# An encoder layer on one core: where the first three right factors of the down projection are rounded

## The chip, the core and the metric

The kernel runs on one core of a Trainium2 chip. A core has TensorE (PE, with its weight loads as PEld), VectorE (DVE), ScalarE (ACT), GpSimd (POOL) and SyncE (SP); SP only issues DMAs here, and POOL mostly does so too. The engines run on their own and wait for each other by semaphores. The metric is the device time of one execution in microseconds, lower is better.

## What is computed

One layer of a streaming encoder, 512 tokens by 2048 channels, all in float32:

```
h = rms_norm(x, pre_mix_g);  z = h @ w_in                 # q, k, v and u
a = chunked_attention(q, k, v, rel_bias);  p = multiscale_pool(u, pool_w, pool_scale)
x = x + rms_norm(concat([a, p]) @ w_o, post_mix_g)
h = rms_norm(x, pre_ffn_g)
up = causal_dwconv(h @ w_up, conv_w, conv_b)              # 2 x 5632 columns
y = (gelu(up[:, :5632]) * up[:, 5632:]) @ w_down          # 5632 x 2048
x = x + rms_norm(y, post_ffn_g)
```

## The kernel before, in words

**Products in parts.** A float32 factor `v` is split into `hi`, which ACT rounds to the type `fp32r` (L140), and `lo = v - hi`, which DVE subtracts (L141). A product is then hi by hi, hi by lo and lo by hi: three matmuls, which `mm3` issues at L162, L164 and L165. Every weight block thus costs a load, a rounding on ACT and a subtraction on DVE before PE can use it.

**Seven products instead of eight.** The w_o product, most of the up projection and the down projection are computed as seven products of sums of quarter blocks. The products are numbered 1 to 7. Product 1 takes the plain block 11 of the weights, 2 and 3 the plain blocks 21 and 22; 5, 7, 6 and 4 take sums of blocks. For the w_o product (`wo_sum`) and for the first part of the down projection (`first_sum`) these sums are made in DRAM by POOL's DMAs long before.

**The down projection** takes 44 row blocks of w_down in five groups c of eight (4 pairs u each), and a last few blocks apart. A group has fourteen products: column half cc = 0 or 1, product i = 1 to 7; each is 24 matmuls of 512 columns. A right factor (cc, i) is a tile of 128 by 2048, 1 MB, split into `bh` and `bl`; a left factor comes from the gated activations that the up projection has stored in DRAM (`gd`), loaded as `gc` (or `a` for the first) and split into `ah` and `al`. The first group's products are taken in the order (0,1), (1,1), (0,2), (1,2), (0,5), ..., and the planner keeps three factors ahead (`AHEAD`).

**The passage** from up to down projection: the last ten products of the up projection run while the first right factors come in. `next_first` is called after the up product 6 of the last half block and after product 4 of the one before it, and each call brings one right factor, (0,1) and (1,1). The right factors' tiles stand in a pool `pr` that is opened when the left sums of the up projection (`h5`, `h3`, `h6`) are dead, with two tiles each of `raw1` (as loaded), `wh` and `wl`; further rings (`later`) come once the up projection's memory is free. One of the two `raw1` tiles holds the last gated activation, `ca`, from the moment its convolution begins until it has been stored to `gd_last[1]`. By the counter of `right_tile`, ring numbers 0 to 3 of `raw1` all come from `pr`.

**What was special of the first three.** (0,1), (1,1) and (0,2) (`READY`) were split amid the w_o products: `ready_blocks` loaded each in two halves (`rw`, L843), rounded them, and stored hi and lo to DRAM (`rw01h` and so on, L850), one step after each quarter of a w_o product other than product 1. At the passage POOL then loaded the finished `bh` and `bl` (L1110); no engine had to split them.

**What sets the order.** PE's order is the program's own. On every other engine a scheduler fixes the order of the instructions when the program is built, by priorities and its own estimates; on the chip each engine then works strictly in that order and waits where it must. Loads on SP also stand in one order.

Of the kernel before, what the change touches and what calls it, by code (L numbers as in the profile page):

```python
# [9 lines left out]
F32 = mybir.dt.float32  # L10
F32R = mybir.dt.float32r
# [4 lines left out]
P = 128  # L16
S = 512
# [14 lines left out]
CU = 4  # L32
# [13 lines left out]
def f32(ap):  # L46
    return ap.bitcast(F32)
# [34 lines left out]
def encoder_layer(ctx: ExitStack, tc: tile.TileContext, x, xT, vecs, rel, post_mix, post_ffn,  # L82
# [7 lines left out]
    nc = tc.nc  # L90
# [7 lines left out]
    dram = ctx.enter_context(tc.tile_pool(name="dram", bufs=1, space=bass.MemoryType.DRAM))  # L98
# [7 lines left out]
    def bank(name):  # L106
        return psum.tile([P, 512], F32, tag="ps", name=name)
# [30 lines left out]
    def split(hi, lo, src, scale=None):  # L138
        if scale is None:
            rounded = nc.scalar.activation(hi, src, AF.Copy)  # L140
            rest = nc.vector.tensor_sub(lo, src, f32(hi))  # L141
        else:
            rounded = nc.scalar.activation(hi, src, AF.Copy, scale=scale)
            rest = nc.vector.scalar_tensor_tensor(lo, src, scale, f32(hi), op0=ALU.mult, op1=ALU.subtract)
        split.last, split.rest = rounded.ins, rest.ins
        return rounded.ins
# [14 lines left out]
    def mm3(ps, l, r, first, last, onto=False):  # L161
        nc.tensor.matmul(ps, l[0], r[0], start=first, stop=False, skip_group_check=onto)  # L162
        low = ps if len(r[1].shape) == 2 else ps.rearrange("p (a b) -> p a b", a=2)
        nc.tensor.matmul(low, l[0], r[1], start=False, stop=False, skip_group_check=onto)  # L164
        nc.tensor.matmul(ps, l[1], r[0], start=False, stop=last, skip_group_check=onto)  # L165
# [41 lines left out]
    def part(w, *idx):  # L207
        return tuple(v[(slice(None),) + idx] for v in w)
# [47 lines left out]
    def first_block(cc, j, l):  # L256
        cs = slice(l * D // 2 + cc * S, l * D // 2 + (cc + 1) * S)
        return w_down[:2 * P * CU, cs].rearrange("(u j p) n -> p u j n", j=2, p=P)[:, :, j, :]

    READY = (0, 1), (1, 1), (0, 2)  # L260
    ready_w = {at: [dram.tile([P, CU, S], F32, name=f"rw{at[0]}{at[1]}{p}") for p in "hl"] for at in READY}

    ready_parts = [(at, j) for at in READY for j in range(2)]

    specs = v_specs(0)
    FIRST_PART = len(specs)
# [21 lines left out]
    first_sum = {i: [dram.tile([P, CU, S], F32, name=f"t{i}{cc}") for cc in range(2)] for i in (5, 7, 6, 4)}  # L288
# [63 lines left out]
    for kb in range(KD):  # L352
        i, o = divmod(kb, 8)
        nc.sync.dma_start(xt[kb // 4][:, kb % 4, :], xT[kb * P:(kb + 1) * P, :])
        for n, what in enumerate("qk"):
            if kb in chunks:
                raw, hi, lo = first[f"{what}0_{i}"]
# [5 lines left out]
        for what in "qk":  # L363
            _, hi, lo = first[f"{what}0_{i}"]
# [248 lines left out]
    with tc.tile_pool(name="p1", bufs=2, reuse_waits="tile") as p1:  # L613
# [222 lines left out]
                split(*(w[:, 4 * i:4 * i + 4, :] for w in parts), v)  # L836
            return parts

        def ready_blocks():
            for at, j in ready_parts:  # L840
                v, hi = (p2.tile([P, 1024], dt, tag=tag, name=tag) for tag, dt in (("rw", F32), ("rwh", F32R)))
                lo = v.bitcast(F32R)
                nc.sync.dma_start(v.rearrange("p (a b) -> p a b", a=2),  # L843
                                  first_block(at[0], at[1] - 1, 0)[:, 2 * j:2 * j + 2, :])
                for _ in range(4):
                    yield
                split(hi, lo, v)
                yield
                for dest, part_ in zip(ready_w[at], (hi, lo)):
                    nc.sync.dma_start(dest[:, 2 * j:2 * j + 2, :], f32(part_).rearrange("p (a b) -> p a b", a=2))  # L850
                for _ in range(3):
                    yield

        ready_steps = ready_blocks()

        wo_banks = [bank(f"m{n}") for n in range(8)]
        ONTO = 6, 3, 7, 4

        def wo_product(i, cc, left, between=None):
            at = 2 * cc + (4 if i in (2, 5, 3) else 0)  # L860
            ps = wo_banks[at:at + 2]
            for q in range(4):
                w = weights.get(f"wo{i}_{cc}_{q}")
                for j in range(2):
                    kb = 2 * q + j
                    for t in range(2):
                        mm3(ps[t], tuple(v[:, kb, t * P:(t + 1) * P] for v in left), part(w, j),
                            i not in ONTO and kb == 0, kb == 7, i in ONTO)
                if i != 1:
                    next(ready_steps, None)  # L870
                if between:
                    between(q)
            return ps
# [9 lines left out]
    with tc.tile_pool(name="p2", bufs=1, reuse_waits="tile") as p2:  # L883
# [38 lines left out]
        for cc in range(2):  # L922
            add_out(y11, cc, wo_product(2, cc, a12))
# [147 lines left out]
    gd_last = [dram.tile([P, 2, S], F32, name=f"gd{u}") for u in (NU - 2, NU - 1)]  # L1071
# [7 lines left out]
    later, turns = {}, {}  # L1079

    def right_tile(tag, name, dt=F32R):

        n = turns[tag] = turns.get(tag, -1) + 1
        if later and n % (2 + LATER[tag]) >= 2:
            return later[tag](name, dt)
        return pr.tile([P, CU, S], dt, tag=tag, bufs=2, name=name)
# [3 lines left out]
    def raw1(name, dt=F32):  # L1090
        return right_tile("raw1", name, dt)

    def right(c, cc):

        def load(j, l):
            b = later["raw2"](f"b{j}{l}") if j else raw1(f"b{j}{l}")
            r, cs = 256 * CU * c, slice(l * C + cc * S, l * C + (cc + 1) * S)
            nc.sync.dma_start(b, w_down[r:r + 256 * CU, cs].rearrange(
                "(u j p) n -> p u j n", j=2, p=P)[:, :, j, :])
            return b  # L1100

        b = {}
        order = yield
        while True:
            i = order
            if (c, (cc, i)) in ready_first:
                hi, lo = right_tile("wh", "bh"), right_tile("wl", "bl")
                for v, source in zip((hi, lo), ready_w[cc, i]):
                    with tc.issue_after(first_right.part) if first_right.part else nullcontext():
                        first_right.part = nc.gpsimd.dma_start(v, source.bitcast(F32R)).ins  # L1110
                order = yield hi, lo
                continue
            if c == 0:

                v = first_right(cc, i, raw1 if (ORDER0.index((cc, i)) - len(ready_first)) % 5 < 3 else later["raw2"])
            else:
                for jl in {1: (11, 12), 6: (22,), 2: (21,)}.get(i, ()):
                    b[jl] = load(jl // 10 - 1, jl % 10 - 1)
                if i == 5:
                    nc.vector.tensor_add(b[11], b[11], b[12])  # L1120
                if i == 7:
                    nc.vector.tensor_add(b[12], b[22], b[12])
                if i == 6:
                    nc.vector.tensor_add(b[11], b[11], b[22])
                if i == 4:
                    nc.vector.tensor_add(b[21], b[21], b[11])  # L1126
                v = b[{1: 11, 5: 11, 7: 12, 6: 11, 2: 21, 3: 22, 4: 21}[i]]
            hi, lo = right_tile("wh", "bh"), right_tile("wl", "bl")
            split(hi, lo, v)
            order = yield hi, lo  # L1130

    def first_right(cc, i, ring):

        v = ring(f"t{i}")
        source = first_sum[i][cc] if i in first_sum else first_block(cc, *{2: (1, 0), 3: (1, 1)}[i])
        with tc.issue_after(first_right.last) if first_right.last else nullcontext():
            first_right.last = nc.sync.dma_start(v, source).ins
        return v

    first_right.last = first_right.part = None  # L1140
    ready_first = [(0, at) for at in READY]

    ORDER = 1, 5, 6, 3, 7, 2, 4
    ORDER0 = tuple((cc, i) for i in (1, 2, 5, 6, 3, 7, 4) for cc in range(2))
# [352 lines left out]
    with tc.tile_pool(name="p4", bufs=2, reuse_waits="tile") as p4:  # L1497
        def ring(tag, shape, n):
            return lambda name, dt=F32: p4.tile([P, *shape], dt, tag=tag, bufs=n, name=name)

        raw2 = later["raw2"] = ring("raw2", (CU, S), 2)
# [66 lines left out]
        def next_product():  # L1568
            c, cc, i, l, r = ready.pop(0)
            multiply(cc, i, l, r)  # L1570
            keep_product(c, cc, i)

        for f in factors():
            ready.append(f)
            if firsts:
                firsts.pop(0)
                with tc.issue_after(split.last):
                    keep_product(0, len(ready) - 1, 1)
            if len(ready) == 2 and product.last is not None:
                with tc.issue_after(first_right.part):  # L1580
                    nc.gpsimd.dma_start(gd_last[1], product.last)
                product.last = None
            if len(ready) > AHEAD:
                next_product()
# [93 lines left out]
        for n in ("11", "12", "21", "22"):  # L1678
            for t in range(2):
                at = y[t + 2 * int(n[0]) - 2]  # L1680
                l = int(n[1]) - 1
                load_sum(n, t, at[:, l * C:(l + 1) * C])
                if n in not_stored:
                    v = at[:, l * C + S:(l + 1) * C]
# [60 lines left out]
```

## Time and profile before

| | us |
|---|---|
| median of 3 timed runs | 1860.05 (1859.49 to 1861.0) |
| the profiled execution, its own time | 1858.89 |
| span of the profiled execution, first to last instruction | 1857.1 |
| PE busy | 1842.6 (99% of the span) |
| DVE busy | 1532.2 (83%) |
| ACT busy | 1084.4 (58%) |
| POOL busy | 302.8 (16%) |
| mean granted clock of PE | 0.999 of full speed |

Times in the trace count from the first instruction. A PE row of 0.39 us does not mean that a matmul takes the array so long: successive matmuls of 512 columns start 0.227 us apart and overlap. "[2.70 <- X]" behind a row is the time for which that engine sat idle before it, and who ended the wait. An idle engine other than PE costs nothing as long as PE does not wait for it.

### The profile page before, as it was taken

How to read it: one execution, taken by the hardware profiler on the slowest of the kernel's cores; microseconds unless marked ns; L12 is line 12 of the kernel's file. 1: busy time of each engine (PE TensorE's matmuls, PEld its weight loads, DVE VectorE, ACT ScalarE, POOL GpSimd, SP SyncE). 2: the span in 40 equal slices, each digit the busy share in tenths (PEclk: the TensorE clock that was granted, in tenths of full speed). 3: DMA queues.
4: the chain of work that ended last, by engine and by line, in shares of the span. 5: the costliest groups of instructions: out<-in, count | busy, mean ns of one | idle time of the engine just before them, and what ended most of it. 6: DMA issues, size and time to landing. Idle time of an engine off the chain costs nothing.

```text
span 1857.1 us, 25452 instructions
## 1 busy us (share of the span) xinstructions
PE 1842.6 (99%) x9598; PEld 1584.3 (85%) x9598; DVE 1532.2 (83%) x1799; ACT 1084.4 (58%) x1376; POOL 302.8 (16%) x402
## 2 busy tenths in 40 slices
PE   9999999999999999999999999999999999999998
PEld 7888888888879888888888888888888888888886
DVE  6988778878588988888887888888887899899876
ACT  7654455456564666566565665666655655565553
POOL 3411001100000112212122122121121001111101
PEclk9999999999999999999999999999999999999999
DMA  8599977998987798888888988889888977777785
GB/s 319 171 319 302 322 230 233 267 264 310 326 308 202 185 220 195 205 204 200 201 200 203 207 202 195 204 206 205 199 179 288 363 224 171 193 211 178 176 230 157
DMA packets 139338, 426.01 MB, mean 229 GB/s; under 512 B 11920, under 2 KB 15376, under 8 KB 133520
## 3 DMA queue, kind: packets, MB, share of 16 engines
q0 software_dynamic: 54864, 173.56, 45.8%
q1 hardware_dynamic: 84352, 250.84, 38.8%
q8 instruction: 75, 1.23, 0.3%
q14 instruction: 47, 0.39, 0.1%
HBM read 370.35 MB, written 104.33 MB: 256 GB/s over the span
## 4 chain that ended last, share of the span: by engine, by line
PE 69%; DMA 1%; DVE 1%; issue 0%; ACT 0%; DVEq 0%; POOLq 0%; ACTq 0%
PE qa L170 16%; PE qa L176 8%; PE qg L170 8%; PE qg L176 4%; PE qd L170 4%; PE pa L162 4%; PE pa L165 4%; PE pa L164 4%; PE qd L176 2%; PE pg L162 2%; PE pg L165 2%; PE pg L164 2%; PE up L165 1%; PE up L162 1%; PE up L164 1%; PE pd L164 1%
## 5 line engine op out<-in xcount | busy, mean ns | idle before, releaser
L140 ACT ACTIVATE wfh<-wx 128x1024 fp32r<-128x1024 f32 x192 | 203.4, 1059 | 154.3 <-PE qg L170 54.4
L170 PE MATMUL qa<-gT,wfh 128*128 128x512 f32 x1152 | 288.6, 392 | 0.0
L141 DVE TENSOR_TENSOR wfl<-wx,wfh 128x1024 fp32r<-128x1024 f32 x192 | 234.6, 1222 | 61.0 <-ACT wfh L140 44.0
L170 PEld LDWEIGHTS qa<-gT,wfh 128*128 128x128 f32 x1152 | 207.2, 189 | 37.1
L1362 POOL DMA_DIRECT2D wx<-in_w_up x122 | 104.6, 858 | 502.6 <-DVE wfl L141 467.9
L140 ACT ACTIVATE wfh<-wy 128x1024 fp32r<-128x1024 f32 x96 | 101.7, 1060 | 108.5 <-PE qg L170 57.2
L170 PE MATMUL qg<-h,wfh 128*128 128x512 f32 x656 | 162.2, 389 | 0.1
L176 PE MATMUL qa<-gT,wfl 128*128 128x256 f32 x1152 | 161.4, 283 | 0.6 <-ACT zm L1422 0.6
L176 PEld LDWEIGHTS qa<-gT,wfl 128*128 128x128 f32 x1152 | 151.5, 191 | 4.9 <-ACT zm L1422 0.8
L170 PEld LDWEIGHTS qg<-h,wfh 128*128 128x128 f32 x656 | 122.9, 188 | 25.9 <-ACT zb L1418 0.5
L141 DVE TENSOR_TENSOR bl<-b,bh 128x2048 fp32r<-128x2048 f32 x56 | 127.2, 2285 | 19.1 <-ACT bh L140 11.7
L140 ACT ACTIVATE bh<-b 128x2048 fp32r<-128x2048 f32 x56 | 106.0, 1911 | 52.8 <-DVE b L1126 21.8
L141 DVE TENSOR_TENSOR wfl<-wy,wfh 128x1024 fp32r<-128x1024 f32 x96 | 117.1, 1220 | 12.6 <-ACT wfh L140 7.8
L162 PE MATMUL pa<-bh,ah 128*128 128x512 f32 x320 | 124.5, 389 | 0.0
L164 PE MATMUL pa<-bl,ah 128*128 128x512 f32 x320 | 124.5, 389 | 0.0
L165 PE MATMUL pa<-bh,al 128*128 128x512 f32 x320 | 124.5, 389 | 0.0
L141 DVE TENSOR_TENSOR wfl<-wz,wfh 128x1024 fp32r<-128x1024 f32 x48 | 58.7, 1223 | 54.2 <-PE qa L170 54.2
L176 PEld LDWEIGHTS qg<-h,wfl 128*128 128x128 f32 x656 | 89.5, 190 | 6.4
L170 PE MATMUL qd<-gT,wfh 128*128 128x512 f32 x384 | 94.9, 389 | 0.0
L176 PE MATMUL qg<-h,wfl 128*128 128x256 f32 x656 | 91.5, 282 | 0.0
L170 PEld LDWEIGHTS qd<-gT,wfh 128*128 128x128 f32 x384 | 71.9, 188 | 14.9
L170 PE MATMUL qa<-h,wfh 128*128 128x512 f32 x328 | 82.1, 392 | 0.0
(554 smaller groups left out, 4352.5 us busy)
## 6 DMA issues: line engine op xcount, KB each, us to landing
wx<-in_w_up POOLq DMA_DIRECT2D x122, 512.0 KB, 6.2
b<-in_w_down SPq DMA_DIRECT2D x32, 1024.0 KB, 7.0
wt<-in_w_o POOLq DMA_DIRECT2D x24, 1024.0 KB, 16.8
wx<-in_w_up SPq DMA_DIRECT2D x43, 512.0 KB, 5.5
wz<-in_w_up SPq DMA_DIRECT2D x41, 512.0 KB, 5.7
wy<-in_w_up SPq DMA_DIRECT2D x41, 512.0 KB, 4.7
wy<-in_w_up POOLq DMA_DIRECT2D x41, 512.0 KB, 6.7
sum<-part POOLq DMA_DIRECT2D x38, 512.0 KB, 6.4
```

The lines of the kernel that those rows point to most:

```text
L140: rounded = nc.scalar.activation(hi, src, AF.Copy)
L141: rest = nc.vector.tensor_sub(lo, src, f32(hi))
L162: nc.tensor.matmul(ps, l[0], r[0], start=first, stop=False, skip_group_check=onto)
L164: nc.tensor.matmul(low, l[0], r[1], start=False, stop=False, skip_group_check=onto)
L165: nc.tensor.matmul(ps, l[1], r[0], start=False, stop=last, skip_group_check=onto)
L170: nc.tensor.matmul(ps, w[0][:, kb], pairs[kb][0], start=fresh and not kb, stop=last, skip_group_check=not fresh)
L176: nc.tensor.matmul(ps[:, sl], w[1][:, kb], pair[:, sl], start=False, stop=last, skip_group_check=not fresh)
L1362: nc.gpsimd.dma_start(self.raw[k, what], self.block(k, m, kh), accum_op=ALU.add)
```

## The change

The three early factors lose their special way. `READY`, `ready_w`, `ready_blocks` and the call in `wo_product` go, with six loads, six roundings, six subtractions and twelve stores of half a factor. At the passage POOL's six loads of finished halves go, and (0,1), (1,1), (0,2) go through `first_right` and `split` like the other eleven: one load of 1 MB on SP, one rounding, one subtraction each. The choice of ring (`raw1` or `raw2`) now counts from the first factor and not from the fourth. The store of the last gated activation no longer stands behind POOL's loads.

```
-    READY = (0, 1), (1, 1), (0, 2)
-    ready_w = {at: [dram.tile([P, CU, S], F32, name=f"rw{at[0]}{at[1]}{p}") for p in "hl"] for at in READY}
...
-        def ready_blocks():
-            for at, j in ready_parts:
-                v, hi = (p2.tile([P, 1024], dt, tag=tag, name=tag) for tag, dt in (("rw", F32), ("rwh", F32R)))
...
-                if i != 1:
-                    next(ready_steps, None)
...
-            if (c, (cc, i)) in ready_first:
-                hi, lo = right_tile("wh", "bh"), right_tile("wl", "bl")
-                for v, source in zip((hi, lo), ready_w[cc, i]):
-                    with tc.issue_after(first_right.part) if first_right.part else nullcontext():
-                        first_right.part = nc.gpsimd.dma_start(v, source.bitcast(F32R)).ins
-                order = yield hi, lo
-                continue
             if c == 0:
-                v = first_right(cc, i, raw1 if (ORDER0.index((cc, i)) - len(ready_first)) % 5 < 3 else later["raw2"])
+                v = first_right(cc, i, raw1 if ORDER0.index((cc, i)) % 5 < 3 else later["raw2"])
...
-        source = first_sum[i][cc] if i in first_sum else first_block(cc, *{2: (1, 0), 3: (1, 1)}[i])
+        source = first_sum[i][cc] if i in first_sum else first_block(cc, *{1: (0, 0), 2: (1, 0), 3: (1, 1)}[i])
...
             if len(ready) == 2 and product.last is not None:
-                with tc.issue_after(first_right.part):
-                    nc.gpsimd.dma_start(gd_last[1], product.last)
+                nc.gpsimd.dma_start(gd_last[1], product.last)
```

PE's order is the same in both programs. Amid the w_o products, on DVE, from the last quarter of product (6,1) on (`wo_..l` is the low part of a w_o block, `y` the product's rows, `small` the norm's statistics, `x` the new residual), before:

```order
L906 TENSOR_TENSOR y_4118<-m_3901,y_4118 128x512
L141 TENSOR_TENSOR rw<-rw,rwh 128x1024
L141 TENSOR_TENSOR wo_0_3l<-wo_0_3r,wo_0_3h 128x1024
L915 TENSOR_TENSOR y_4118<-y_4118,gain 128x2x512
L952 TENSOR_REDUCE small<-small 128x2
```

and after:

```order
L882 TENSOR_TENSOR y_4112<-m_3895,y_4112 128x512
L141 TENSOR_TENSOR wo_0_3l<-wo_0_3r,wo_0_3h 128x1024
L891 TENSOR_TENSOR y_4112<-y_4112,gain 128x2x512
L928 TENSOR_REDUCE small<-small 128x2
L929 TENSOR_SCALAR small<-small 128x2
```

The subtraction `rw` that stood between the product's addition and the next low part is gone; the rest keeps its order.

SP's queue at the passage, before (`t` is a right factor as loaded, `gc` and `a` left factors; the digit behind `t` is the product):

```order
L1455 DMA a_13117<-gd0_0_5654 128x4x256
L1137 DMA t2_13308<-in_w_down 128x4x512
L1521 DMA gc0_13299<-gd0_0_5654 128x2048
L1137 DMA t5_13318<-t50_108 128x2048
L1521 DMA gc1_13324<-gd0_1_5655 128x2048
```

and after:

```order
L1423 DMA a_13071<-gd0_0_5606 128x4x256
L1106 DMA t1_13065<-in_w_down 128x4x512
L1106 DMA t1_13107<-in_w_down 128x4x512
L1106 DMA t2_13251<-in_w_down 128x4x512
L1489 DMA gc0_13257<-gd0_0_5606 128x2048
L1106 DMA t2_13266<-in_w_down 128x4x512
L1106 DMA t5_13276<-t50_102 128x2048
L1489 DMA gc1_13282<-gd0_1_5607 128x2048
```

Three loads, (0,1), (1,1) and (0,2), now stand ahead of (1,2)'s and of both loads of left factors `gc`.

DVE's queue at the passage, before (`z` and `RR` belong to the up projection's results, `ca`, `cb`, `cx` to the convolution):

```order
L141 TENSOR_TENSOR al<-a,ah 128x1024
L1437 TENSOR_TENSOR z<-qa_12801,z 128x256
L1438 TENSOR_TENSOR z<-z,RR 128x1024
L1427 TENSOR_TENSOR zm<-zb,zm 128x512
L1207 SCALAR_TENSOR_TENSOR ca<-z,vec,ca 128x511 x2
L1208 SCALAR_TENSOR_TENSOR ca<-z,vec,ca 128x510 x2
```

and after, two pieces (rows between them left out by "..."):

```order
L141 TENSOR_TENSOR al<-a,ah 128x1024
L1405 TENSOR_TENSOR z<-qa_12753,z 128x256
L1406 TENSOR_TENSOR z<-z,RR 128x1024
L141 TENSOR_TENSOR bl<-t_13065,bh 128x2048
L1175 SCALAR_TENSOR_TENSOR ca<-z,vec,ca 128x511 x2
...
L1406 TENSOR_TENSOR z<-z,RR 128x1024
L141 TENSOR_TENSOR bl<-t_13107,bh 128x2048
L1175 SCALAR_TENSOR_TENSOR cb<-z,vec,cb 128x511
...
L1198 TENSOR_TENSOR ca<-ca,cx 128x512
L141 TENSOR_TENSOR bl<-t_13251,bh 128x2048
L141 TENSOR_TENSOR al<-gc_13257,ah 128x1024
L141 TENSOR_TENSOR bl<-t_13266,bh 128x2048
```

Three subtractions of 2048 columns now stand among the last convolutions, and `al` of the second left factor stands behind the third of them; the three roundings stand at the same places of ACT's queue.

## Rows read from the trace of the kernel before

**Rows 1.** The page, its first part: busy time of each engine, share, instructions.

```profile
PE 1842.6 (99%) x9598; PEld 1584.3 (85%) x9598; DVE 1532.2 (83%) x1799; ACT 1084.4 (58%) x1376; POOL 302.8 (16%) x402
```

**Rows 2.** PE's waits from 380 us on: line, waited for: us in total, times, longest.

```profile
PE m L164 <- DVE wo_1l L141: 2.7, 1, 2.7
PE pd L164 <- DMA bl<-rw02l: 0.6, 1, 0.6
PE qa L176 <- ACT zm L1422: 0.6, 1, 0.6
```

**Rows 3.** Order of time, PE: start us, us, line, out<-in [idle before].

```profile
518.91 0.50 PE L164 MATMUL m<-wo_1l,s 128*128 128x512 f32 x1 [2.70 <-DVE wo_1l L141]
```

**Rows 4.** The same, ACT and then DVE, ahead of that wait.

```profile
505.93 1.06 ACT L140 ACTIVATE rwh<-rw 128x1024 fp32r<-128x1024 f32 x1 [5.84 <-DMA rw<-in_w_down]
...
507.02 1.23 DVE L141 TENSOR_TENSOR rw<-rw,rwh 128x1024 fp32r<-128x1024 f32 x1 [4.36 <-ACT rwh L140]
...
512.86 4.86 DVE L967 SCALAR_TENSOR_TENSOR x<-y,small,x 128x1024 f32<-128x1024 f32 x4
517.64 1.21 DVE L141 TENSOR_TENSOR wo_1l<-wo_1r,wo_1h 128x1024 fp32r<-128x1024 f32 x1
```

**Rows 5.** By tile: the removed pieces, duration ns min/median/max, first and last start.

```profile
L140 ACT ACTIVATE rwh<-rw x6: 1059/1061/1062, 424.5 to 505.9; 128x1024 fp32r<-128x1024 f32 x6
L141 DVE TENSOR_TENSOR rw<-rw,rwh x6: 1219/1226/1229, 425.6 to 507.0; 128x1024 fp32r<-128x1024 f32 x6
...
L1110 POOL DMA_DIRECT2D bh<-rw01h x1: 817/817/817, 1404.3 to 1404.3; - x1
```

**Rows 6.** By tile: the added pieces' kind, as eleven other factors have it.

```profile
L140 ACT ACTIVATE bh<-t x11: 1900/1917/1933, 1429.4 to 1478.8; 128x2048 fp32r<-128x2048 f32 x11
L141 DVE TENSOR_TENSOR bl<-t,bh x11: 2280/2285/2293, 1431.5 to 1484.1; 128x2048 fp32r<-128x2048 f32 x11
```

**Rows 7.** Order of time, ACT and DVE at the passage.

```profile
1415.19 0.39 ACT L1436 ACTIVATE z<-qa 128x256 f32<-128x256 f32 x1 [0.83 <-PE qa L170]
...
1416.78 1.23 DVE L1438 TENSOR_TENSOR z<-z,RR 128x1024 f32<-128x1024 f32 x1
```

**Rows 8.** Order of time, PE: the first down products (0,1), (1,1), (0,2), (0,5).

```profile
1423.29 0.39 PE L162 MATMUL pa<-bh,ah 128*128 128x512 f32 x1
...
1428.96 0.39 PE L164 MATMUL pa<-bl,ah 128*128 128x512 f32 x1
...
1435.49 0.39 PE L165 MATMUL pd<-bh,al 128*128 128x512 f32 x1
...
1446.41 0.39 PE L165 MATMUL pg<-bh,al 128*128 128x512 f32 x1
```

**Rows 9.** DMA issues, each of one short stretch: KB, median us to landing.

```profile
b<-in_w_down SPq DMA_DIRECT2D x1, 1024.0 KB, 5.8
...
DMA to landing us min/median/max: 5.8/7.0/9.8
...
b<-in_w_down SPq DMA_DIRECT2D x1, 1024.0 KB, 6.7
gc<-gd SPq DMA_DIRECT2D x1, 1024.0 KB, 8.7
...
t<-t SPq DMA_DIRECT2D x1, 1024.0 KB, 4.8
...
t<-in_w_down SPq DMA_DIRECT2D x1, 1024.0 KB, 10.5
```

**Rows 10.** By stretch: us, busy of PE, PEld, DVE, ACT, POOL, clock, DMA, GB/s.

```profile
1411.00:1420.00 9.00, 9.00 (x50) 7.81 (x49) 7.16 (x10) 4.62 (x7) 0.00 (x0) 1.00 1.06 419
```

**Rows 11.** The same, at PE's one wait amid w_o and behind its last matmul.

```profile
516.00:519.00 3.00, 0.30 (x2) 0.09 (x1) 3.00 (x4) 0.76 (x2) 0.00 (x0) 1.00 0.80 259
...
1852.00:1857.00 5.00, 0.00 (x0) 0.00 (x0) 1.68 (x4) 0.00 (x0) 0.00 (x0) 0.50 0.58 210
```

## What I predict

> **What bounds the kernel now.** I read the page's busy times first: TensorE works for 1842.6 us of a span of 1857.1 [rows 1]. A change can therefore do two things: fill what little PE still waits, or make PE wait anew. The list of PE's waits from the w_o products to the end has three lines: 2.7 us for `wo_1l`, 0.6 for the stored `bl` of (0,2), 0.6 for `zm` in the up projection [rows 2]. The change touches the first two. All it can win is thus 2.7 + 0.6 = 3.3 us, 0.18% of the time. What it can lose has no such limit, so most of the working is about the passage.
>
> **The w_o products: what goes.** In order of time PE stands still for 2.70 us before the second matmul on `wo_1l`, up to 518.91 [rows 3]. Followed backwards [rows 4]: DVE made `wo_1l` at 517.64, directly behind the new residual `x`, which it began at 512.86 and which took 4.86 us. DVE had come late to `x`, since it had waited 4.36 us for `rwh`, and ACT 5.84 us for the last half factor `rw` from DRAM. Both engines work strictly in their order, so ACT's rounding `rwh` of 1.06 us and DVE's subtraction `rw` of 1.23 held up all that was queued behind them. The new order lacks both. DVE's work behind them then begins at once; the wait of 4.36 and the 1.23 of the piece itself go, of which the other waits of the norm take back a little: I put `wo_1l` some 5 us earlier, at 512.5. PE needs it at 518.91 − 2.70 = 516.2. The margin of 3.7 us makes the wait vanish whole: **−2.7 us**. If something else were last there, between 0 and 2.7 would be kept; the top is excluded from being more, since no other wait stands there.
>
> The other pieces removed are six roundings of 1.06 us and six subtractions of 1.23 us, spread from 424.5 to 507 [rows 5], six loads and twelve stores on SP and six loads on POOL. I cost them at nothing: PE's list shows no wait near them but the one just counted, so PE's own products cover them; the stores gate nobody but POOL's loads at the passage.
>
> **The passage: what comes.** Three roundings of 1.92 us on ACT, three subtractions of 2.29 us on DVE (the duration of eleven other factors' [rows 6]) and three loads of 1 MB on SP. As 4.2 us of engine work per factor beside products of 24 × 0.227 = 5.4 us this would hide. What matters is where loads may start. `pr` has two `raw1` tiles. One holds `ca` until the last gated activation is stored. So (0,1), (1,1) and (0,2), ring numbers 0, 1 and 2, all come through the other tile, and each load must wait until DVE's `bl` of the factor before has read it. SP works in order, so the load of `gc0`, which stands behind (0,2)'s, waits as well. It is a chain of load, rounding, subtraction, load, rounding, subtraction.
>
> *Factor (0,1).* POOL's load of its stored half started at 1404.3, when the up projection's memory was free [rows 5]; I take no later a start for the new load. With any landing time of the rows below it is there ahead of ACT's place for it, behind `z` at 1415.19 [rows 7]: rounded by 1417.5. DVE's place for it is behind the addition that starts at 1416.78 and takes 1.23: `bl` from 1418.0 to 1420.3. PE takes it at 1423.29 [rows 8], so it costs nothing; 3 us of margin.
>
> *Load time.* This is the one large unknown: L, from issue to landing of 1 MB from w_down on SP. The kernel loads the same tiles all through the down projection: alone 5.8 us at the least, 7.0 in the median, up to 9.8 [rows 9]. One load of another source landed after 4.8, and the load of (1,2) at the passage took 10.5 [rows 9], in a stretch in which DMA moved 419 GB/s [rows 10]. That traffic was largely POOL's 6 MB of stored halves, which the change takes away, and at 1420 and 1430 only one load is open, because the next may not start. I take 5.9; ends 4.8 and 10.5.
>
> *Factor (1,1).* Load from 1420.3 to 1426.2, `bh` to 1428.1, `bl` to 1430.4. PE's second matmul of the product wants `bl` at 1428.96 [rows 8]: **1.4 us** of wait, part of the next sum.
>
> *Factor (0,2).* Load from 1430.4 to 1436.3, `bh` to 1438.2, `bl` to 1440.5. The left factor `gc0` is queued directly behind; in the pair of rows where a 1 MB load and a `gc` follow each other they took 6.7 and 8.7 us [rows 9], so it lands some 2.4 us after the factor, 1438.7, and `ah` is ready at 1439.8, `al` behind DVE's `bl` at 1441.6. Before, the third matmul of that product, the first to use `al`, ran at 1435.49 [rows 8]. Thus **+6.1 us** in all, the 1.4 included and the old 0.6 for `rw02l` replaced. In L the sum is 1420.3 + 2 L + 9.5, so each microsecond of L counts twice.
>
> *Factors (1,2) and (0,5).* They no longer wait for one slot; loads of 1 MB then land some 2.5 us apart. (1,2) lands near 1441.5 and is rounded by 1443.6, 2 us ahead of its product. Behind it DVE has two `bl`, three pieces of 1024 columns and two of 512 before the `al` of (0,5): 4.6 + 3.7 + 1.4 = 9.7, so 1453.3 less overlaps of 0.1 each, 1452.8 to 1453.1. Due is the row of 1446.41 [rows 8] plus 6.1 = 1452.5: about **+0.5 us**. From there PE takes 5.4 us a factor while ACT, DVE and the loads need 2 to 4.6, so the lead is rebuilt and nothing is late again. ca's convolution ends some 4 us later on DVE, but its consumer, a later product, is no earlier due.
>
> **The clock.** With the new waits PE does almost nothing from about 1435.7, the end of (1,1)'s product, to 1439.9, and runs two matmuls until 1441.6. [...] Hence +1.5 in place of +0.5.
>
> **Sum.** −2.7 + 6.1 + 1.5 = **+4.9 us**. The profiled execution had 1858.89 and its span 1857.1; it would come to 1863.8. It lies 1.2 below the median of the runs, 1860.05, so the forecast on that scale is **1865.0 us**.
>
> [...] The rows give 5.8 to 5.9 us for an undisturbed load of 1 MB [rows 9]. [...]
>
> **The rivals.**
> - *The clock holds.* The two matmuls between and the short gaps keep it at 1.00. −2.7 + 6.1 + 0.5 = +3.9: 1864.0. For it: the 2.70 us at 516 did nothing. Against: this gap is longer. Chance 0.22.
> - *Quick loads.* One row shows 4.8 us [rows 9]. With L = 4.8 the stall is 6.1 − 2 × 1.1 = 3.9, and PE's gap shrinks to that of 516, which left the clock alone: −2.7 + 3.9 = +1.2, 1861.3. [...] For quick loads: DMA is nearly idle then. Against: not one of the w_down loads came under 5.8. Chance 0.14.
> - *The other side: the stall is hidden.* If loads of (1,1) and (0,2) need not wait for DVE's `bl`, because the slot is free earlier than I think, all three land ahead of PE and only the gains stay: −2.7 to −3.3, 1857.4 to 1856.8. It decides where L falls to 5.9 − 3.4 / 2 = 4.2 us, where stall and gain are equal. Against: two tiles, `ca` in one. Chance 0.06, and most of it lies within 0.2%.
> - *The w_o wait stays.* If another load or the norm's own chain makes `wo_1l` late, the 2.7 is not won: +7.6, 1867.6. Chance 0.08. The change not doing what it says would be this case too.
> - *Dear loads.* At the median of 7.0 [rows 9] the stall grows by 2.2: +7.1, 1867.1. At the 10.5 of the passage's own load it grows by 9.2: +14.1, 1874. For it: the row of 10.5 was taken in this very stretch. Against: its company is gone. Chance 0.10.
>
> **How the numbers follow.** The forecast with the clock falling has 0.40; the five rivals 0.22, 0.14, 0.06, 0.08 and 0.10. A measurement of this kernel tells 0.2%, 3.7 us, from no change: below 1856.3 is faster, above 1863.8 slower. Faster needs more than the gains that exist, so 0.03 for what I have not seen. Slower: the forecast (its price of the clock could be 0 and L 5.8, so 0.34 of its 0.40), 0.15 of the 0.22 that the clock holds, the last two whole, and little else: 0.68. Same: 0.29. The range runs from 1861.0, which cuts off the hidden stall and half of the quick loads, to 1868.5, which takes in the w_o wait and loads of 7 us and cuts off the dearest.
>
> **What the profile after would show.** PE's wait for `wo_1l` near 516 is gone. SP's loads of `t1` start near 1404 and 1420.3 and the first of `t2` near 1430.4, each directly at the end of a `bl`, with 5.8 to 6 us to landing. PE waits about 1.4 us for the `bl` of (1,1), then 4 to 5 us for `ah` and `al` of `gc0`. The clock by stretches reads less than 1.00 a little behind 1440. I am wrong if the load of (1,1) starts before 1420 (another slot), if L is far from 5.9, or if PE's wait at 516 has a new releaser.

## The result and the profile after

The changed kernel takes 1866.9 us in the median (1863.93 to 1869.13, 6 runs), the kernel before beside it 1860.37. The ratio is 1.0035 with an interval of 1.0022 to 1.0047: **slower by 6.5 us**, where +4.9 was forecast (1865.0, range 1861.0 to 1868.5). A second set of runs (after_again below) gave 1.0018 (1.0008 to 1.0028), 1864.23 against 1860.65. One execution of each of the two kernels in that set took 3085 us, at a mean granted clock of 0.556, and is left out of the ratio. Slower holds in both sets; the size is less certain, since the two intervals together reach from 1.5 to 8.7 us.

The profiled execution took 1866.7, its span is 1864.9 against 1857.1. The page's first part, to set beside [rows 1]:

```profile
PE 1847.7 (99%) x9598; PEld 1587.5 (85%) x9598; DVE 1533.1 (82%) x1796; ACT 1084.4 (58%) x1373; POOL 300.7 (16%) x396
```

PE has the same 9598 matmuls and is busy 5 us longer: a first sign that they ran slower, since no work was added. PE's waits from 380 us on, to set beside [rows 2]:

```profile
PE pd L162 <- ACT ah L140: 3.4, 1, 3.4
PE pa L164 <- DVE bl L141: 1.8, 1, 1.8
PE pd L165 <- DVE al L141: 0.6, 1, 0.6
PE pg L165 <- DVE al L141: 0.4, 1, 0.4
PE qa L176 <- ACT zm L1390: 0.3, 1, 0.3
```

The wait for `wo_1l` is gone; four new ones stand at the first down products. In order of time, PE at the place of [rows 3] and at those of [rows 8]:

```profile
516.13 0.40 PE L164 MATMUL m<-wo_1l,s 128*128 128x512 f32 x1
...
1419.99 0.39 PE L162 MATMUL pa<-bh,ah 128*128 128x512 f32 x1
...
1427.87 0.50 PE L164 MATMUL pa<-bl,ah 128*128 128x512 f32 x1 [1.82 <-DVE bl L141]
...
1438.43 0.50 PE L162 MATMUL pd<-bh,ah 128*128 128x512 f32 x1 [3.44 <-ACT ah L140]
...
1439.76 0.79 PE L165 MATMUL pd<-bh,al 128*128 128x512 f32 x1 [0.61 <-DVE al L141]
...
1441.21 0.63 PE L165 MATMUL pd<-bh,al 128*128 128x512 f32 x1
...
1445.05 0.63 PE L165 MATMUL pd<-bh,al 128*128 128x512 f32 x1
...
1454.20 0.50 PE L165 MATMUL pg<-bh,al 128*128 128x512 f32 x1 [0.39 <-DVE al L141]
```

DVE began `wo_1l` 5.2 us earlier than in [rows 4]:

```profile
512.43 1.22 DVE L141 TENSOR_TENSOR wo_1l<-wo_1r,wo_1h 128x1024 fp32r<-128x1024 f32 x1
```

PE reaches (0,1) 3.3 us earlier than before (1423.29) and the third matmul of (0,2) 4.3 later (1435.49). The rows 1441.21 and 1445.05 are nine matmuls apart, 0.427 us each and not 0.227; the granted clock reads 0.50 there, as the steps from 1440 on show below. The third matmul of (0,5) is 7.8 later (1446.41), and so it stays to the end.

The chain behind these waits, in ACT's and DVE's rows of the same stretch:

```profile
1423.57 1.92 ACT L140 ACTIVATE bh<-t 128x2048 fp32r<-128x2048 f32 x1 [2.60 <-DMA t<-in_w_down]
...
1434.34 1.91 ACT L140 ACTIVATE bh<-t 128x2048 fp32r<-128x2048 f32 x1 [7.44 <-DMA t<-in_w_down]
1437.32 1.06 ACT L140 ACTIVATE ah<-gc 128x1024 fp32r<-128x1024 f32 x1 [1.07 <-DMA gc<-gd]
...
1414.63 2.29 DVE L141 TENSOR_TENSOR bl<-t,bh 128x2048 fp32r<-128x2048 f32 x1
...
1425.53 2.29 DVE L141 TENSOR_TENSOR bl<-t,bh 128x2048 fp32r<-128x2048 f32 x1 [2.23 <-ACT bh L140]
...
1436.28 2.29 DVE L141 TENSOR_TENSOR bl<-t,bh 128x2048 fp32r<-128x2048 f32 x1 [4.62 <-ACT bh L140]
1438.49 1.22 DVE L141 TENSOR_TENSOR al<-gc,ah 128x1024 fp32r<-128x1024 f32 x1
```

The first `bl` ends at 1416.9, the second at 1427.8. SP's loads of (1,1) and (0,2) were issued at 1416.94 and 1427.84, each at the end of the `bl` before it. SP's own waits from 1385 to 1436 us name the same releaser for both; below that line stands their time to landing, each load taken in a short stretch:

```profile
SPq L1106 <- DVE bl L141: 19.9, 2, 15.6
...
t<-in_w_down SPq DMA_DIRECT2D x1, 1024.0 KB, 6.6
...
t<-in_w_down SPq DMA_DIRECT2D x1, 1024.0 KB, 6.5
```

And the granted clock (the third figure from the end) in steps of 5 us: it fell twice, behind the wait of 1.8 us and behind the long one.

```profile
1425.00:1430.00 5.00, 3.17 (x11) 2.06 (x10) 4.47 (x5) 1.90 (x3) 0.00 (x0) 0.88 0.13 32
1430.00:1435.00 5.00, 4.98 (x18) 3.68 (x16) 1.67 (x3) 0.66 (x1) 0.56 (x1) 0.78 0.99 295
1435.00:1440.00 5.00, 0.96 (x3) 0.61 (x4) 3.43 (x2) 3.28 (x4) 0.00 (x0) 0.91 1.00 380
1440.00:1445.00 5.00, 5.00 (x12) 3.89 (x13) 2.01 (x1) 3.95 (x4) 0.00 (x0) 0.50 1.03 434
1445.00:1450.00 5.00, 5.00 (x21) 4.04 (x20) 3.03 (x3) 0.73 (x1) 0.00 (x0) 0.91 1.02 429
```

### The profile page after: what moved, and what is told of

The parts are those of the page before. It is cut to its first block, busy times and chain, and to the rows that moved or that the text cites. A ratio compares the mean times of both kernels' runs of the same rounds, so it can differ in the third digit from the quotient of the medians.

```text
span 1864.9 us, 25394 instructions
## 1 busy us (share of the span) xinstructions
PE 1847.7 (99%) x9598; PEld 1587.5 (85%) x9598; DVE 1533.1 (82%) x1796; ACT 1084.4 (58%) x1373; POOL 300.7 (16%) x396
## 4 chain that ended last, share of the span: by engine, by line
PE 93%; DMA 3%; DVE 2%; ACT 1%; issue 1%; SPq 0%; DVEq 0%; POOLq 0%; ACTq 0%
PE qa L170 18%; PE qa L176 10%; PE qg L170 9%; PE qg L176 5%; PE qd L170 4%; PE pa L165 4%; PE pa L164 4%; PE pa L162 4%; PE m L162 3%; PE m L165 3%; PE m L164 3%; PE qd L176 2%; PE pg L165 2%; PE pg L164 2%; PE pg L162 2%; PE v L164 2%
```

## The experiments

All of them are read by the same three distances between PE's rows in the trace, in us: the w_o products (first to last matmul), (0,1) (its first matmul) to (0,2) (its third), and from there to the third matmul of (0,5). Without a wait and at a granted clock of 1.00 they are 158.7 (after), 11.3 (two_stored) and 10.9 (before). What lies ahead of them is left out: PE's first w_o matmul stands between 389.3 and 392.6 us in these fourteen traces, so spans of single traces differ by up to 3.4 us before the change can tell. Beside them the timed median, that of the kernel before in the same set, and the ratio with its interval.

| kernel | w_o | to (0,2) | to (0,5) | median, before | ratio |
|---|---|---|---|---|---|
| before | 161.6 | 12.2 | 10.9 | | |
| before_again | 164.9 | 11.8 | 10.9 | 1859.85, 1860.94 | 0.9994 (0.9980 to 1.0007) |
| after | 158.7 | 19.8 | 14.4 | 1866.9, 1860.37 | 1.0035 (1.0022 to 1.0047) |
| after_again | 158.7 | 19.0 | 12.5 | 1864.23, 1860.65 | 1.0018 (1.0008 to 1.0028) |
| wo_alone | 158.7 | 15.4 | 10.9 | 1859.09, 1860.62 | 0.9999 (0.9986 to 1.0012) |
| wo_alone_2 | 158.7 | 15.8 | 12.3 | 1854.62, 1860.65 | 0.9975 (0.9965 to 0.9985) |
| passage_alone | 164.0 | 19.1 | 13.6 | 1869.71, 1860.62 | 1.0050 (1.0036 to 1.0064) |
| other_ring | 158.7 | 14.4 | 11.6 | 1858.0, 1860.62 | 0.9989 (0.9979 to 0.9999) |
| no_link | 158.7 | 14.7 | 11.6 | 1860.13, 1860.62 | 0.9999 (0.9990 to 1.0008) |
| two_links | 158.7 | 14.7 | 13.2 | 1859.81, 1860.65 | 0.9999 (0.9991 to 1.0008) |
| in_pieces | 158.7 | 13.1 | 11.6 | 1856.82, 1860.94 | 0.9973 (0.9963 to 0.9984) |
| clock_held | 158.7 | 19.2 | 12.4 | 1862.96, 1860.65 | 1.0014 (1.0005 to 1.0023) |
| two_stored | 160.2 | 11.3 | 11.5 | 1854.64, 1860.94 | 0.9960 (0.9942 to 0.9977) |
| two_stored_lead | 158.7 | 11.3 | 11.5 | 1855.84, 1861.57 | 0.9970 (0.9959 to 0.9981) |

**The two halves of the change, each alone.** First the w_o part, on the kernel before:

```
-                if i != 1:
-                    next(ready_steps, None)
...
-                for v, source in zip((hi, lo), ready_w[cc, i]):
+                for v, source in zip((hi, lo), [first_block(cc, i - 1, 0)] * 2):
```

> One part of the change alone. The loads, roundings, subtractions and stores of the three factors amid the w_o products are gone, the passage is as before: POOL loads six finished halves (it reads w_down unsplit as both halves, so the values of the three first down products are not the layer's, the work is). My theory: the only thing won in the w_o products is PE's wait of 2.70 us for wo_1l, and it is not given back later, so 1860.4 - 2.7 to 3.0 = 1857.4 to 1857.7. The rival that the wait comes back elsewhere (the up projection, the passage): 1860.4. PE's list of waits tells them apart: no wait near 516, and 0.6 us for bl at the passage as before.

The w_o products took their 158.7 us, but the passage lost 3.2 to two waits that the edit itself brought, and the time is that of before:

```profile
PE pa L164 <- DMA bl<-in_w_down: 1.8, 1, 1.8
PE pd L164 <- DMA bl<-in_w_down: 1.7, 1, 1.7
```

So its time, where 1857.4 to 1857.7 was expected, tells nothing of the sum. It was repeated with `(first_sum[5][cc], first_sum[6][cc])` as sources:

> Again the w_o part alone, with the fault of wo_alone mended: there POOL read the rows of w_down in pieces and came late (waits of 1.8 and 1.7 us for bl that the kernel before hasn't). Here it reads whole tiles of the same layout as the stored halves (the sums t5 and t6, so the values of the three first down products are not the layer's). My theory: no wait at 516, 0 to 0.6 us of wait at the passage, 2.7 to 3.3 us below the kernel before. Rival (the gain of the w_o products is given back): no difference.

The ratio of 0.9975 is 4.6 us, the medians lie 6.0 apart: more than forecast, although the profiled execution of this kernel, one of its slowest, waited 4.0 us for POOL's last load. The other half, the passage of the changed kernel with the early steps still in place:

```
-                v = first_right(cc, i, raw1 if (ORDER0.index((cc, i)) - len(ready_first)) % 5 < 3 else later["raw2"])
+                v = first_right(cc, i, raw1 if ORDER0.index((cc, i)) % 5 < 3 else later["raw2"])
...
-    ready_first = [(0, at) for at in READY]
+    ready_first = []
...
```

> The other part alone. The three factors are still loaded, rounded, subtracted and stored amid the w_o products (nobody reads the stores), and the passage is that of the changed kernel. My theory: the two parts add up, so the wait of 2.7 us at 516 stands and the passage costs the same as in the changed kernel: 1866.9 + 2.7 to 3.0 = 1869.6 to 1869.9. Rival: the passage's loss depends on what was won before (the clock or the loads fall differently): 1866.9 or less. Also looked at: the granted clock behind the 2.70 us wait at 516, against the clock behind the wait of 1.8 us at the passage.

It came to 1869.7, as said. Its 9.3 us (ratio 1.0050) less 4.6 are 4.7, between the two measurements of the whole: within the noise of these sets the two halves add up. Its waits show both:

```profile
PE pd L162 <- ACT ah L140: 5.0, 1, 5.0
PE m L164 <- DVE wo_1l L141: 3.1, 2, 2.7
PE pa L164 <- DVE bl L141: 1.5, 1, 1.5
PE m L164 <- DVE wo_3l L141: 0.7, 1, 0.7
```

**The kernel before, looked at again.**

> The kernel before once more, with a profile. wo_alone_2 had most of its runs near 1854, some 6 us below the kernel before, while only 2.7 to 3.3 us were to be won in the w_o products; but its profiled run, one of its slowest, lost 4.0 us at the passage waiting for POOL's last load, the bl of (0,2). My theory: the kernel before loses to that same load in most of its runs more than the 0.6 us of the one trace, by chance of when POOL's loads land; then this profile shows a wait there of 1 to 5 us, and the time of the run goes with it (floor near 1857, plus the wait). Rival: the wait is 0.6 us again and the spread comes from elsewhere.

The rival was right: 0.2 us at the passage. What differs lies in the w_o products, 164.9 us and not 161.6. PE waited as long for `wo_1l`, but this time the clock fell behind it (the second row, 0.68):

```profile
519.68 0.75 PE L164 MATMUL m<-wo_1l,s 128*128 128x512 f32 x1 [2.75 <-DVE wo_1l L141]
...
515.00:520.00 5.00, 1.92 (x10) 1.18 (x9) 5.00 (x5) 1.54 (x2) 0.00 (x0) 0.98 0.70 225
520.00:525.00 5.00, 5.00 (x18) 3.97 (x18) 4.66 (x7) 1.13 (x2) 0.00 (x0) 0.68 0.94 354
```

The early steps thus cost 2.9, 5.3 and 6.2 us in the three traces that have them all, while every trace without them has 158.7. The one trace that I predicted from had the smallest loss. That agrees with wo_alone_2; how much of the spread of the kernel before (1855 to 1867 over the sets) comes from this stays open, since none of its slowest runs was profiled.

**The serial loads.** One index takes (0,2) to the other ring:

```
-                v = first_right(cc, i, raw1 if ORDER0.index((cc, i)) % 5 < 3 else later["raw2"])
+                v = first_right(cc, i, raw1 if (ORDER0.index((cc, i)) + 1) % 5 < 3 else later["raw2"])
```

> The changed kernel with one index shifted, so that the load of (0,2) goes to the other ring (raw2) and no longer waits for DVE's bl of (1,1) in the one free raw1 tile. By the program its load then waits for the last product of the up projection, near 1420. My theory (serial loads through one tile): the wait for ah and al of gc0, 3.4 and 0.6 us, and the second fall of the clock, some 2.8 us, vanish; the wait of 1.8 us for bl of (1,1) and the fall of the clock behind it (1.7) stay. So 1860.4 - 3.3 + 2.2 + 1.7 = 1861.0, without that fall 1859.3. Rival (the loads of this stretch are slow whichever tile they go to, or ACT and DVE are what is late): within 1 us of 1866.9.

This is the test of the main claim, and it held: the load of (0,2) was issued at 1422.37 and not behind the `bl` of (1,1), the long wait is gone, and the kernel is at least as fast as before (1858.0, where 1859.3 was expected without a fall of the clock). Of the short waits that for `al` did not vanish. Left are

```profile
PE pa L164 <- DVE bl L141: 1.3, 1, 1.3
PE pd L165 <- DVE al L141: 0.6, 1, 0.6
```

and three waits of 0.3 to 0.4. The clock stayed at 1.00 at the passage. Next both links were cut, (1,1) loaded straight into its `bl` tile:

```
+            if c == 0 and (cc, i) == (1, 1):
+                hi, lo = right_tile("wh", "bh"), right_tile("wl", "bl")
+                nc.gpsimd.dma_start(lo, first_block(cc, 0, 0).bitcast(F32R))
+                split(hi, lo, f32(lo))
+                order = yield hi, lo
+                continue
```

> The changed kernel, with (1,1) loaded by POOL straight into its bl tile and split in place, so that it needs no raw1 tile; (0,2) then gets a tile of the later ring by the counter. Both links of the chain are gone: the load of (1,1) starts near 1404, that of (0,2) near 1420. My theory: all three are split ahead of PE, PE waits nowhere and the clock stays at 1.00: 1860.4 - 2.7 - 0.6 = 1857.1. If the load of (0,2) lands after 6.6 us or more, up to 1 us of wait for al of gc0: 1858. Rival (rounding and subtraction at the passage are themselves what is late): 1862 or more.

The wait at (1,1) went, but (0,2) now waited 2.3 us for `bl` and 0.6 for `al`, and the time was that of before: expectation missed. I thought of the load, which stood behind the last up product (issued at 1421.07), and gave (0,2) the tile of (0,1) with one line more, `turns["raw1"] += 1`:

> As no_link ((1,1) loaded by POOL straight into its bl tile), but the counter of raw1 is moved on by one, so that (0,2) takes the tile that (0,1) had, right behind DVE's bl of (0,1), and not a tile of the later ring, which waits for the last product of the up projection. The load of (0,2) starts near 1417 and lands near 1423.5; bh 1425.5, bl 1428, al of gc0 near 1430, PE wants it near 1432. My theory: no wait of PE at (1,1) and (0,2), clock 1.00 throughout, only what was won in the w_o products stays: 2.7 to 3.3 us below the kernel before. Rival (some other work of ACT or DVE in this stretch is late): within 1 us of the kernel before, like no_link.

The load came at 1416.31, 3.0 us ahead of PE's first down matmul and no longer 0.2 behind it, and nothing changed: the expectation was missed again. Its rows, ACT, then DVE, then PE, say why:

```profile
1427.26 1.91 ACT L140 ACTIVATE bh<-t 128x2048 fp32r<-128x2048 f32 x1
...
1421.92 2.29 DVE L141 TENSOR_TENSOR bl<-bl,bh 128x2048 fp32r<-128x2048 f32 x1 [0.85 <-ACT bh L140]
1424.12 0.42 DVE L1412 TENSOR_TENSOR z<-qa,z 128x256 f32<-128x256 f32 x1
...
1429.99 0.68 DVE L1205 TENSOR_TENSOR ca<-ca,cx 128x512 f32<-128x512 f32 x1
1430.59 2.29 DVE L141 TENSOR_TENSOR bl<-t,bh 128x2048 fp32r<-128x2048 f32 x1
1432.79 1.22 DVE L141 TENSOR_TENSOR al<-gc,ah 128x1024 fp32r<-128x1024 f32 x1
...
1432.93 0.50 PE L164 MATMUL pd<-bl,ah 128*128 128x512 f32 x1 [2.27 <-DVE bl L141]
```

No row waits for a load. DVE takes the `bl` of (1,1) ahead of the last `z` and, in its fixed order, the `bl` of (0,2) only behind the last convolution; between those two it is idle for 0.89 us, in one wait for ACT's `cb`. This is the rival that I had not priced: **the three added subtractions fill DVE**, and with the loads out of the way DVE's queue is the next thing late, by 2.9 us. Subtracting (0,2) in four pieces, `al` behind the first of them, tests it:

```
+                pieces.extend((lo[:, u], v[:, u], f32(hi[:, u])) for u in range(CU))
+                nc.vector.tensor_sub(*pieces.pop(0))
...
+                            while pieces:
+                                with tc.issue_after(first_split[1]):
+                                    nc.vector.tensor_sub(*pieces.pop(0))
```

> As two_links, where no load was late any more but PE still waited 2.3 us for bl and 0.6 for al at (0,2), since DVE had the subtractions behind the last convolution. Here DVE subtracts (0,2) in four pieces of 512 columns: one, then al of gc0, then the other three. My theory (DVE's queue is what is late): bl's first piece is ready 1.6 us earlier, al 1.6 us earlier, the sum of waits falls from 2.9 to about 1.3 us and the time by 1.6 us against two_links, 1858 to 1858.5. Rival (something else than DVE's queue sets the start of (0,2)): waits as in two_links.

```profile
1432.40 0.50 PE L164 MATMUL pd<-bl,ah 128*128 128x512 f32 x1 [0.66 <-DVE bl L1110]
1433.53 0.50 PE L165 MATMUL pd<-bh,al 128*128 128x512 f32 x1 [0.64 <-DVE al L141]
```

The waits fell from 2.9 to 1.3 us as forecast: the queue it was. The median of 1856.82 (0.9973) is lower still than the 1858 to 1858.5 expected. In the traces half of the difference from two_links is the clock, which fell there to 0.50 behind the waits at (0,2) and stayed at 1.00 here (13.2 and 11.6 us to (0,5)).

**The clock.** Useless matmuls in the gaps, in the changed kernel:

```
+    FILL, filler = {(1, 1): 7, (0, 2): 20}, []
...
+        for k in range(FILL.pop((cc, i), 0)):
+            nc.tensor.matmul(ps[k % 2], filler[0][0][:, 0, :P], filler[0][1][:, 0], start=True, stop=True)
+        filler[:] = [(l[0], r[0])]
```

> The changed kernel once more, beside the next three on the same chip, and a second profile of it. My theory: again some 6.5 us above the kernel before; waits of 1.5 to 1.8 us for bl of (1,1) and 4 to 5 us for ah and al at (0,2); the clock falls behind the long wait, as it did in the trace of the passage alone; whether it falls behind the short one too (it did in the first trace of this kernel, not in the passage alone, where the wait was 1.5) is open. Rival: the fall behind the short wait belongs to this kernel and comes again.

> The changed kernel with useless matmuls where PE waits: 7 ahead of product (1,1), 20 ahead of product (0,2), into the product's own banks, which the product then overwrites. The loads, roundings and subtractions come no earlier, only the clock has less reason to fall. My theory: the second fall (14 matmuls at half speed, 2.9 us) is a cost by itself, and a fall behind the short wait is hidden in the long wait that follows; so the time is that of after_again less 2.9: +3.6 on the kernel before, and the granted clock at (0,2) is 1.00. Rivals: the clock's price is hidden elsewhere: no gain; both falls cost: less 4.5.

after_again came 3.6 us above the kernel before and not 6.5. Its clock did not fall behind the short wait (1.26 us) but did behind the long one (5.0), for seven matmuls; in clock_held it read 1.00 throughout. The two traces reach the third matmul of (0,2) at the same time, 1438.11 and 1438.08. The five intervals from there took 2.20 us in after_again and 1.26 in clock_held, and yet both reach the third matmul of (0,5) nearly together, at 1450.65 and 1450.43. So in this pair the fall cost 0.2 us, not the 0.9 of its slow matmuls. With the clock held PE ran into a longer wait for `al` of (0,5):

```profile
PE pg L165 <- DVE al L141: 0.8, 1, 0.8
```

against 0.41 in after_again. DVE would have been late anyway. The saving of 2.9 us that was expected did not come, and the rival of a hidden price fits: the medians lie 1.3 apart, with intervals that overlap.

In the first trace of the changed kernel the second fall lasted longer, from 1439 to 1445.5, and its fourteen slow matmuls took 3.0 us more than at full clock. There it reached DVE: the addition of `pd`, which stands in DVE's order ahead of the next `bl` and of the `al` of (0,5), had to wait for PE, as it did not in the other two traces:

```profile
1447.25 0.69 DVE L1148 TENSOR_TENSOR part<-pd,part 128x512 f32<-128x512 f32 x1 [1.97 <-PE pd L165]
```

From (0,2) to (0,5) this trace took 14.4 us and clock_held 12.4, so the fall cost some 2 us, and most of the other 1.5 is DVE's queue. two_links and no_link, with the same waits, differ by 1.6 there (13.2 and 11.6), and only the first had a fall.

**A version that beats both.** Only (0,1) and (1,1) stored early, (0,2) split at the passage:

```
-    READY = (0, 1), (1, 1), (0, 2)
+    READY = (0, 1), (1, 1)
...
-                v = first_right(cc, i, raw1 if (ORDER0.index((cc, i)) - len(ready_first)) % 5 < 3 else later["raw2"])
+                v = first_right(cc, i, raw1 if ORDER0.index((cc, i)) % 5 < 3 else later["raw2"])
```

> The kernel before with only two early factors, (0,1) and (1,1), split amid the w_o products, and only (0,2) loaded and split at the passage, with the ring index of the changed kernel. It tells whether the loss is the serial chain or the passage's splitting as such: one factor alone finds a raw1 tile free when the up projection's memory is (load at 1404 in the times of before), DVE's bl of it stands behind the last convolution at 1430.4, al of gc0 ends at 1433.9, PE wants them at 1435.2 and 1435.5. The last early step in the w_o products comes earlier by 30 us, so the norm isn't held up. My theory: no wait at 516, none at the passage, POOL's late load of the third bl gone too: 1854 to 1857.5. Rival (ACT and DVE can't take even one more split here): a wait for bl or al of 1 us or more, 1858 or more.

1854.64, ratio 0.9960 (0.9942 to 0.9977). All that PE still waits for:

```profile
PE m L164 <- DVE wo_1l L141: 0.9, 1, 0.9
PE pg L165 <- DVE al L141: 0.4, 1, 0.4
```

One factor's load finds a free tile and one subtraction fits into DVE's queue. The 0.9 stands at 473.78, behind the last early step. The last experiment gave the loads of these steps more time (`range(4)` to `range(7)` quarters between load and split):

> As two_stored, but each half factor is split seven quarters of a w_o product after its load was asked for, not four. In the traces a load of rw starts only when the store of the part before it has landed, and ACT then stands 3 to 8 us at the rounding, with all that is queued behind it; in two_stored PE still lost 1.5 us near 474 to that. My theory (what the early splitting costs is this wait of ACT in its queue, not its 1.06 and 1.23 us of work): that wait is gone, PE waits nowhere in the w_o products, 1.5 us below two_stored: 1853.1. Rival (the work itself delays the norm, wherever it stands): PE waits there as before, 1854.6 or more.

Its trace did what was said: no wait in the w_o products and a span of 1853.6, 1.1 below two_stored's. The timed runs don't show it (1855.84), and the two intervals overlap; so the mechanism is seen, the gain isn't.

## Why the prediction was right, step by step

- **The w_o wait.** Right in place and cause: `wo_1l` was ready at 513.65 at the latest (it started at 512.43; I had 512.5), and PE went through. That 512.5 was the start of the subtraction and not its end, so the margin was 2.5 us and not the 3.7 that I gave. Mis-sized: I took 2.7 us from one trace. That trace had 2.9 in all; two others had 5.3 and 6.2, since further waits of 0.2 to 0.7 and once a fall of the clock come with it.
- **Other removed work at nothing.** Right: without the steps the w_o products take 158.7 us in every trace, so no other wait was behind that work.
- **(0,1) in time.** Right; PE did not wait. Its load was issued at 1395.08, earlier than the 1404 that I took.
- **The chain.** Right: both loads were issued at the end of the `bl` before, and other_ring took the long wait away by one index. Read by the letter, my sign of being wrong, a load of (1,1) ahead of 1420, was met by 1416.94. But it was no other slot: I had left the sign in the times of before, and the `bl` that the load waited for ended at 1416.92.
- **The load time.** Mis-sized: L was 6.6 and 6.5 and not 5.9, so the chain is 1.3 us longer; with the 3.3 us by which PE was earlier, 1441.6 becomes 1438.3, and 1439.76 was measured, 1.5 later. My 5.9 lay near the least of rows whose median was 7.0 [rows 9], and the rival of 7.0 was nearer in this trace. "Only one load is open" held for (1,1), which took 6.6 all the same; behind the load of (0,2) four more were issued within 3 us. In after_again L was 5.8 and 6.5. The quick loads of 4.8 us did not appear: no load on this chain landed under 5.8, and on POOL's path the load of (1,1) in two_links took 6.4.
- **(0,5).** +0.5 forecast; 0.4 of wait measured behind the slow matmuls, 0.8 where the clock was held.
- **The clock.** Right that it falls behind the long gap, to 0.50 in both traces of the kernel and in passage_alone. Missed: in the first trace it fell behind the wait of 1.8 us, too; that fall (1.6 us of slow matmuls) vanished in the long wait behind it. No run shows the 1.5 that my sum has for the clock in place of the 0.5 of (0,5): it was my estimate, and the 1.0 by which it is more lies between the two prices that the runs showed, 0.2 net (after_again against clock_held) and some 2 (after).
- **The sum.** In the trace +7.8 against +4.9: 1.5 more from L and the wait behind it, 2.0 more between (0,2) and (0,5), where the clock and DVE's queue together took 3.5 and not 1.5, 0.6 less since PE came 3.3 and not 2.7 us earlier. In the timed runs +6.5 and +3.3 by the two ratios. The forecast lies between them, and that is partly luck, because two errors of size cancel: the gain in the w_o products is larger than 2.7 (2.9, 5.3 and 6.2 in three traces, 4.6 by wo_alone_2), and so is the loss at the passage (9.3 by passage_alone against 7.6).
- **The rival that was missing** is DVE's queue. I had said that 4.2 us of work per factor would hide beside 5.4 us of products. It would on average, but the additions stand ahead of work with a due time. It didn't decide here, since the loads were later still; it decided once they were not, by 2.9 us in two_links.

## What to carry to other kernels

A pool of two tiles of which one was held made the loads serial here, and (1,1) cost its whole landing time of 6.6 us plus 4.3 of the work that empties the tile; look at who holds each slot before calling a load prefetched. Behind the first wait that was removed stood the next engine's fixed order, with 2.9 us of waits in two_links: read the rows ahead of the late instruction, not only what it waits for. And one trace shows one draw of a wait on a DMA: the early steps cost 2.9 us in one trace of the kernel before and 6.2 in the other. Where a gain is read from a single wait, a second profile of the same kernel shows how far it spreads.

## What the hardware showed that I had not expected

How long PE waited did not by itself tell whether the clock fell. Behind 1.82 us (after), 2.27 (two_links) and 2.75 (before_again) it went to 0.50; behind 1.84 (wo_alone), 2.26 (no_link), 2.70 (before, [rows 3, 11]) and 2.74 (passage_alone) it stayed at 1.00. For the pair at nearly the same wait, two_links and then no_link:

```profile
1435.00:1438.00 3.00, 3.00 (x9) 2.35 (x8) 1.21 (x1) 0.65 (x1) 0.00 (x0) 0.50 0.82 287
...
1435.00:1438.00 3.00, 2.44 (x11) 2.02 (x12) 2.71 (x2) 2.27 (x2) 0.00 (x0) 1.00 0.99 418
```

All four of 3.4 us or more, in after, wo_alone_2 (4.0), after_again and passage_alone (5.0), brought a fall to 0.50.
